# Sixteen experts as four rounds of four, in plain fp32 on 32-column tiles of the tensor engine

## The chip, the cores and the metric

The kernel runs on one core of a Trainium2 chip. A core has five engines that work side by side, each through its own instructions in the order in which the program gives them: TensorE (PE; its weight loads stand as PEld), VectorE (DVE), ScalarE (ACT), GpSimd (POOL) and SyncE (SP). Transfers between HBM and the on-chip memory are issued by SP, POOL and ACT and carried out by 16 DMA engines. The metric is the device time of one execution in microseconds (us).

## What is computed

One encoder layer on x of 512 tokens by 1024, all float32. First x grows by two mixers (attention and a bidirectional state space model, through w_in, w_attn_o, w_ssd_o and w_out); then by a mixture of 16 experts on the normed tokens h2:

```
h2 = rmsnorm(x, norm_ffn_w)
# a router takes one of 4 groups, and in it 2 of 4 experts, for each token
for e in range(16):
    y_e = (silu(t @ w1[e]) * (t @ w3[e])) @ w2[e]     # 1024 -> 512 -> 1024
    out = out + combine[:, e:e + 1] * y_e
```

Each token has two experts, so the 16 experts have 64 tokens each on average. The kernel gives every expert a list of CAP = 96 places; a general path behind the stage serves experts with more tokens, and it is skipped here. The experts' weights are 96 MB of float32: 192 pieces of 512 KB.

## The kernel before

**Order.** All work up to the end of the expert stage is written as jobs, `job(engine, us, emit, after, take, free, prio)`, of the class Plan (L122 to L210). Plan.run (L171) puts them in order on a model of the engines: each job has a time, a load has 1.0 us more (DLAT), two engines are 0.2 us apart (LAT), and rooms are counted ("e" for weights, "G" for gathered tokens, "whl" for split weights, "ys" for results). Of the jobs of an engine, the one that can start earliest goes next, and among equals the one of the lowest prio. The order that comes out is the program; on the chip each engine keeps it and waits at any instruction whose inputs are late, whatever stands behind it.

**Precision.** A float32 product is made of three passes in the faster type fp32r: a weight piece is split by ACT into a rounded high part (L1333) and by DVE into the rest (L1337), tokens likewise (L1628, L1632), and mm3 (L266) multiplies high by high, high by low, low by high (L267 to L269).

**The expert stage**, one expert after another. The stationary operand is the tokens' 128 x 96 block, the moving one a 128 x 512 block of weights. up_mm makes u = t @ w1 and v = t @ w3 (8 blocks of 128 rows each), g_silu and g_mul make the gated product, q_mmt transposes it, down_mm makes y (4 blocks, two halves of 512). An expert has 24 such products of three passes, 72 matmuls of 512 columns; the stage has 1152. Each expert's weights are 12 pieces, and the planner keeps the u and v of an expert ahead of the down product of the one before.

**Tokens.** h2 is stored to HBM (h2_d, L1406, four transfers of 512 KB by POOL). The first two experts' tokens come by a product with one-hot lists (pg_first, L1473); those of the other 14 by an indirect gather of 96 rows on POOL (L1620) into one of NG = 3 rooms, and eight transposes of a block on PE (L1625). Lists come from s_oh, s_mm, s_ix (L1601 to L1613). The results go out by an indirect scatter that adds to HBM (L1676, 16 of 96 rows), from a single room.

**Weights** are loaded by SP (eload, L1682) into 18 rooms of their own, 3 of an older pool and 12 in the places of tiles that are done with (`more`, L1704); a room is free when its piece has been split. w1 and w3 pieces have rows of 2 KB, w2 pieces of 4 KB.

Of the kernel before, what the change touches and what calls it, by code (L numbers as in the profile page):

```python
# [11 lines left out]
F32 = mybir.dt.float32  # L12
F32R = mybir.dt.float32r
BF16 = mybir.dt.bfloat16
I32 = mybir.dt.int32
# [22 lines left out]
# numbers of buffers  # L38
# [16 lines left out]
# model of the engines: delay between two, after a load; between dependent steps of one  # L55
# [8 lines left out]
ONEHOT = 2  # L64
TG = ((0, 2), (2, 3), (3, 4))
WARM = 36
# interval of the tensor engine's clock, load of an activation table
# [10 lines left out]
PGP = (320, 2015)  # L78
PGB = (('sc', 'sc'), ('tp', 'tp'))
# [30 lines left out]
class Late:  # L110
    """a tile that takes its buffer at its first use"""
# [10 lines left out]
class Plan:  # L122
    """jobs of one engine each, put in order on a model of the engines (time of a job, a delay between engines,
    buffers that jobs take and give back); of the jobs that can start, the one of the lowest prio goes first"""
# [36 lines left out]
    def clock(self, t, us, duty):  # L161
        """the end of a job of the tensor engine: at half its clock in an interval that follows an idle one"""
# [51 lines left out]
def tile_block(ctx: ExitStack, tc: tile.TileContext, x, norm_mix_w, w_in, b_gate, q_norm_w, k_norm_w,  # L214
# [18 lines left out]
    # ---------------------------------------------------------------- helpers  # L233
# [16 lines left out]
    def rsqrt(y, v, n, eps=EPS):  # L250
        """steps of a reciprocal square root"""
# [19 lines left out]
    # ---------------------------------------------------------------- x, constants  # L271
# [9 lines left out]
    def a2(nm, dt=F32, pat=None, **kw):  # L281
# [4 lines left out]
                 "a2": NA2 - 6, "eb": 3, "ab": 2, "a4": 2, "qa": 3, "cbm": 2, "gat": 0, "e": 0, "u": 2, "H": 2, "Q": 1, "G": NG, "ys": 1, "sl": 1})  # L286
# [18 lines left out]
    # ---- loads of the first part, in the order in which they are needed  # L305
# [27 lines left out]
    def warm(n):  # L333
        """keeps the clock of the tensor engine up"""
# [67 lines left out]
    # ---- first norm  # L402
# [54 lines left out]
    # ---- token-major projections: keys, values, step sizes; queries  # L457
# [75 lines left out]
    # ---- constants  # L533
# [4 lines left out]
    def rope_w():  # L538
        """steps of the factors of the rotation, with the weights of the norms and the scale of the scores in them"""
# [21 lines left out]
    rc = cp.tile([P, NT, NE, 5], BF16, name="rc")  # L561
# [3 lines left out]
    def router_c():  # L565
        V.tensor_copy(rc[:, :, :, 0:2],
                      cst[:, C_TC:C_TC + 8].rearrange("p (t j) -> p t j", j=2).unsqueeze(2).to_broadcast([P, NT, NE, 2]))
# [10 lines left out]
    # ---- norm and rotation of queries and keys  # L578
# [45 lines left out]
    # ---------------------------------------------------------------- from the other projections to the merge  # L624
# [11 lines left out]
    # ---- stream of weights: 128 output channels at a time  # L636
# [101 lines left out]
    # ---- step sizes, decays  # L738
# [79 lines left out]
    # ---- keys  # L818
# [36 lines left out]
    # ---- the projections themselves  # L855
# [25 lines left out]
    # ---- SSD states  # L881
# [43 lines left out]
    # ---- SSD outputs  # L925
# [37 lines left out]
    def ssd_dt(c, d):  # L963
        """x times its step size, per direction"""
# [132 lines left out]
    # ---- attention  # L1097
# [123 lines left out]
    # ---- gates, merge  # L1221
# [31 lines left out]
    # ---- buffers of the second half: a part takes the room of an earlier one when that is done  # L1253
# [7 lines left out]
    def room_q():  # L1261
# [4 lines left out]
        t_["s"] = ep.tile([P, DE], F32, tag="s", name="s_e")  # L1266
# [8 lines left out]
    # ---------------------------------------------------------------- second residual, norm, router  # L1275
# [9 lines left out]
    def room(i, *shapes):  # L1285
        """parts of a tile of the router's room"""
# [12 lines left out]
    sqj_, lgs, oh0a, oh0b, beat, pr, wn, lg, mx5, sm5, go, df, wsum, gv = room(  # L1299
        1, [256], [2 * P], [NT, CAP], [NT, CAP], [NT * 5, 4, 4], [NT * 5, 4], [NT * 5, 4], [NT, 20], [NT * 5], [NT * 5], [NT, 4],  # L1300
# [4 lines left out]

    def oh0(e):
        return (oh0a, oh0b)[e]()
# [20 lines left out]
    def piece(nm, prio, load, k, n, take, give, deps, sp):  # L1328
        """a piece of weights: its load and its two parts"""
# [47 lines left out]
    def logits(t, kb):  # L1377
        """channels in four column groups of the tensor engine, to be summed"""
# [36 lines left out]
    def topk(t0, t1):  # L1415
        """steps of the choice of a group and of two experts in it, for a range of tokens"""
# [33 lines left out]
    # position of every token in every expert's list: routed tokens upwards from 0, the others downwards from S - 1  # L1450
# [13 lines left out]
    # tokens of the first experts, by a matrix product with their one-hot slots  # L1464
    def oh_first(e, t):
        V.tensor_tensor(oh0(e)[:, t, :], iota[:, :CAP], slot[:, t, e:e + 1].to_broadcast([P, CAP]), op=ALU.is_equal)

    def pg_first(e, t, kb):
        if t == 0:
            t_["pg", e, kb] = bank(PGB[e][kb], "pg%d_%d" % (e, kb))  # L1470
            T.matmul(t_["pg", e, kb], lhsT=onb, rhs=zb[:, 0:1].to_broadcast([P, 512]), start=True, stop=False)
        for j in range(4):
            T.matmul(t_["pg", e, kb][:, j * P:j * P + CAP], lhsT=us(t)[:, (kb * 4 + j) * P:(kb * 4 + j + 1) * P],  # L1473
                     rhs=oh0(e)[:, t, :], start=False, stop=(t, j) == (NT - 1, 3))

    # weight of every token for every expert, in exact bf16 parts
    def weigh():
# [3 lines left out]
        def w3(a):  # L1481
            return a.unsqueeze(2).to_broadcast([P, NT, NE])
        return [(0.14, lambda: V.tensor_tensor(cw, prv()[:, :, 4:20], mk, op=ALU.mult)),
# [410 lines left out]
```

## Time and profile before

| | us |
|---|---|
| median of 3 runs (lowest, highest) | 691.66 (691.45, 691.82) |
| span of the profiled execution | 691.8 |
| expert stage, first to last matmul | 389.7 to 677.8 |
| PE busy in the stage | 287.7 |
| last matmul to the end | 14.0 |

No time of its own is given for the profiled execution beyond its span; the span agrees with the runs to 0.1 to 0.3 us. A page of the profile gives busy time by engine, then the span in 40 slices of 17.3 us; a slice's digit is the busy share in tenths. The clock row shows which share of full speed TensorE was granted, the DMA row the mean share of the 16 DMA engines. Timeline rows give start, duration, engine, line, operation and operands of each instruction, and in brackets the idle time before it with what ended it.

### The profile page before, as it was taken

How to read it: one execution, taken by the hardware profiler on the slowest of the kernel's cores; microseconds unless marked ns; L12 is line 12 of the kernel's file. 1: busy time of each engine (PE TensorE's matmuls, PEld its weight loads, DVE VectorE, ACT ScalarE, POOL GpSimd, SP SyncE). 2: the span in 40 equal slices, each digit the busy share in tenths (PEclk: the TensorE clock that was granted, in tenths of full speed). 3: DMA queues.
4: the chain of work that ended last, by engine and by line, in shares of the span. 5: the costliest groups of instructions: out<-in, count | busy, mean ns of one | idle time of the engine just before them, and what ended most of it. 6: DMA issues, size and time to landing. Idle time of an engine off the chain costs nothing. (4 is left out here: it accounts for less than half of the span.)

```text
span 691.8 us, 10208 instructions
## 1 busy us (share of the span) xinstructions
PE 669.1 (97%) x3609; PEld 517.9 (75%) x3611; DVE 553.7 (80%) x877; ACT 463.2 (67%) x689; POOL 96.5 (14%) x118
## 2 busy tenths in 40 slices
PE   7899999999999999999999999999999999999991
PEld 5788887777888888888777877777777777777761
DVE  4679968978699996566526899999999999999981
ACT  5445555777568779433435478888888888888870
POOL 4624100222000000000012102011111111100001
PEclk9999999999999999999999999999999999999996
DMA  8721732565221012897638999999999999999613
GB/s 278 195 65 38 178 90 66 151 182 124 61 62 40 24 51 67 278 340 259 252 118 278 366 357 338 367 375 365 363 363 361 362 361 359 362 377 376 244 23 48
DMA packets 96043, 155.04 MB, mean 224 GB/s; under 512 B 8680, under 2 KB 45044, under 8 KB 95988
## 3 DMA queue, kind: packets, MB, share of 16 engines
q1 hardware_dynamic: 87076, 131.79, 55.3%
q0 software_dynamic: 6848, 22.49, 12.8%
q8 instruction: 29, 0.48, 0.3%
q10 hardware_dynamic: 2064, 0.07, 0.2%
q14 instruction: 26, 0.21, 0.1%
HBM read 143.74 MB, written 10.58 MB: 223 GB/s over the span
## 5 line engine op out<-in xcount | busy, mean ns | idle before, releaser
L267 PE MATMUL b<-hTh,wc_hi 128*128 128x512 f32 x208 | 85.3, 410 | 0.0
L269 PE MATMUL b<-hTh,wc_lo 128*128 128x512 f32 x208 | 82.1, 395 | 0.0
L268 PE MATMUL b<-hTl,wc_hi 128*128 128x512 f32 x208 | 82.1, 395 | 0.0
L657 ACT ACTIVATE wc_hi<-wc_r 128x1024 fp32r<-128x1024 f32 x34 | 35.9, 1057 | 29.8 <-PE b L268 16.3
L661 DVE TENSOR_TENSOR wc_lo<-wc_r,wc_hi 128x1024 fp32r<-128x1024 f32 x34 | 41.5, 1223 | 8.8 <-ACT wc_hi L657 8.5
L1676 POOL DMA_INDIRECT out_dram<-GY,ixe x16 | 27.9, 1746 | 144.1 <-ACT GY L1673 138.4
L267 PEld LDWEIGHTS b<-hTh,wc_hi 128*128 128x128 f32 x208 | 39.0, 188 | 10.4 <-issue 1.5
L269 PEld LDWEIGHTS b<-hTh,wc_lo 128*128 128x128 f32 x208 | 39.0, 187 | 9.5
L268 PEld LDWEIGHTS b<-hTl,wc_hi 128*128 128x128 f32 x208 | 39.1, 188 | 7.7
L1337 DVE TENSOR_TENSOR whl<-ve_r,whl 128x1024 fp32r<-128x1024 f32 x25 | 30.6, 1223 | 3.9 <-ACT whl L1333 3.0
L1333 ACT ACTIVATE whl<-ve_r 128x1024 fp32r<-128x1024 f32 x25 | 26.5, 1058 | 8.5 <-PE pue L269 8.5
L1337 DVE TENSOR_TENSOR ue_lo<-ue_r,ue_hi 128x1024 fp32r<-128x1024 f32 x24 | 29.3, 1221 | 3.1 <-ACT ue_hi L1333 2.9
L1620 POOL DMA_INDIRECT GY<-h_d,ixe x14 | 14.4, 1026 | 117.5 <-PE pge L1625 99.1
L1333 ACT ACTIVATE ue_hi<-ue_r 128x1024 fp32r<-128x1024 f32 x24 | 25.3, 1055 | 3.5 <-PE y1e L269 2.6
L1337 DVE TENSOR_TENSOR whl<-ue_r,whl 128x1024 fp32r<-128x1024 f32 x21 | 25.6, 1221 | 1.0 <-ACT whl L1333 1.0
L1333 ACT ACTIVATE whl<-ue_r 128x1024 fp32r<-128x1024 f32 x21 | 22.3, 1061 | 6.1 <-PE y1e L269 4.1
L1337 DVE TENSOR_TENSOR we_lo<-we_r,we_hi 128x1024 fp32r<-128x1024 f32 x21 | 25.6, 1221 | 0.7
L267 PE MATMUL pve<-whl,H 128*96 128x512 f32 x64 | 26.1, 408 | 0.0
L1333 ACT ACTIVATE we_hi<-we_r 128x1024 fp32r<-128x1024 f32 x21 | 22.3, 1062 | 5.6 <-PE pve L269 4.5
L267 PE MATMUL pue<-whl,H 128*96 128x512 f32 x64 | 25.9, 404 | 0.0
L1157 DVE TENSOR_TENSOR PTl<-ppt,PTh 128x512 fp32r<-128x512 f32 x32 | 21.6, 687 | 4.8 <-ACT PTh L1152 4.5
L267 PE MATMUL pue<-ue_hi,H 128*96 128x512 f32 x64 | 25.3, 396 | 0.0
(400 smaller groups left out, 2069.9 us busy)
## 6 DMA issues: line engine op xcount, KB each, us to landing
ue_r<-in_w_dram SPq DMA_DIRECT2D x45, 512.0 KB, 12.2
ve_r<-in_w_dram SPq DMA_DIRECT2D x44, 512.0 KB, 9.8
we_r<-in_w_dram SPq DMA_DIRECT2D x39, 512.0 KB, 12.3
wc_r<-in_w_in_dram SPq DMA_DIRECT2D x26, 512.0 KB, 5.0
EXx<-in_w_dram SPq DMA_DIRECT2D x22, 512.0 KB, 12.2
EXm<-in_w_dram SPq DMA_DIRECT2D x22, 512.0 KB, 11.7
EXr<-in_w_dram SPq DMA_DIRECT2D x20, 512.0 KB, 12.7
x<-in_x_dram SPq DMA_DIRECT2D x8, 512.0 KB, 6.8
```

What stands on the lines that cost most here:

```text
L267: T.matmul(ps, lhsT=lh, rhs=rh, start=first, stop=False)
L268: T.matmul(ps, lhsT=lh, rhs=rl, start=False, stop=False)
L269: T.matmul(ps, lhsT=ll, rhs=rh, start=False, stop=last)
L657: A.activation(t_["w", i][0], t_["raw", i], AF.Copy)
L661: V.tensor_tensor(l_, t_.pop(("raw", i)), h_.bitcast(F32), op=ALU.subtract)
L1157: V.tensor_tensor(PTl[:, :, q2], t_.pop(("pt", u)).rearrange("p (k q) -> p k q", k=NT), PTh[:, :, q2].bitcast(F32), op=ALU.subtract)
L1333: A.activation(t_["w", nm][0], t_["raw", nm], AF.Copy)
L1337: V.tensor_tensor(l_, t_.pop(("raw", nm)), h_.bitcast(F32), op=ALU.subtract)
L1620: G.indirect_dma_start(g[:n], None, h2_d, bass.IndirectOffsetOnAxis(ap=t_["ix", nm][:n, 0:1], axis=0))
L1676: G.indirect_dma_start(out, bass.IndirectOffsetOnAxis(ap=t_["ix", nm][:n, 0:1], axis=0), y_buf()[:n], None, compute_op=ALU.add)
```

## The change

A round q (four of them) takes four experts at once, 4*j+q for j = 0 to 3, each in a 32-column tile j of the tensor engine: the stationary operand is 32 tokens of expert j (RN = 32), the moving operand a raw float32 block of its weights, and the output the partitions 32j to 32j+31 of one bank. Each list of 96 has NR = 3 parts r, so a block of weights of four experts is passed three times. A job of up_mm or down_mm is four such plain matmuls. Per round there are 24 jobs for u, 24 for v and 12 for each half of y: 288 in all. Nothing is split: L1333 and L1337 go from the stage, the tokens' splits too, and one copy (t_out, s_out) takes the place of each pair. A group of four weight rooms is freed by the last part's job (spent) instead of by a split. All pieces have rows of 2 KB; the w2 pieces are halves of the output's columns. Rooms are 35 (18, 3, two in EXm, four each in EXx, EXr and the new EXu).

The stage's order is a list of 16 phases, in which u of a round is put ahead of y of the round before. Only part (0, 0) comes by one-hot products; the other 11 parts come by gathers of 128 rows into NG = 2 rooms, taken in turn, and 12 scatters of 128 rows leave from three rooms. The transposes of round q have the prio just below v of round q-1.

```diff
 NE4 = 18
-NG = 3
...
+NG = 2
...
+RN = 32
+NR = CAP // RN
+NQ = 4
...
+    def oh_first(t):
+        V.tensor_tensor(oh0()[:, t, :].rearrange("p (j i) -> p j i", j=4), iota[:, 0:RN].unsqueeze(1).to_broadcast([P, 4, RN]),
+                        slot[:, t, :].rearrange("p (j q) -> p j q", q=NQ)[:, :, 0:1].to_broadcast([P, 4, RN]), op=ALU.is_equal)
+    def pg_first(t, kb):
         if t == 0:
...
+            t_["pg", kb] = bank("sc", "pg%d" % kb)
+            T.matmul(t_["pg", kb], lhsT=onb, rhs=zb[:, 0:1].to_broadcast([P, 512]), start=True, stop=False)
         for j in range(4):
...
+            T.matmul(t_["pg", kb][:, j * P:(j + 1) * P], lhsT=us(t)[:, (kb * 4 + j) * P:(kb * 4 + j + 1) * P],
+                     rhs=oh0()[:, t, :], start=False, stop=(t, j) == (NT - 1, 3))
...
+    pgj = {0: [], 1: []}
+    for t in range(NT):
+        j_ = job("dve", 0.17, lambda t=t: oh_first(t), [j_slot[t]], prio=PGP)
+        for kb in range(2):
+            pgj[kb] = [job("pe", 1.0 + 0.22 * (t == 0), lambda t=t, kb=kb: pg_first(t, kb), [j_, j_us[t]] + pgj[kb],
+                           ["sc"] if t == 0 else [], prio=PGP, duty=0.9)]
...
+    ohp = [cp.tile([P, NT, P], BF16, name="oh_%d" % i) for i in range(NR)]
+    TH = [Late(h8, "TH%d" % i, F32, "p (a k s) -> p a k s", a=2, k=KD) for i in range(NR)]
+    GS = [Late(a8, "GS%d" % i, F32, "p (a n) -> p a n", a=2) for i in range(2)]
+    YS = [Late(lambda nm, i=i: whl.tile([P, 1024], F32, tag=("hi", "lo")[i % 2], name=nm), "YS%d" % i) for i in range(4)]
+    def T_(q, r):
+        i = (q % 2) * NR + r
+        return TH[i // 2][:, i % 2]
+    def g_buf(R):
+        return GS[0][:, R % NG, :]
+    def y_buf(r):
+        return YS[r][:, :]
+    def s_buf(r):
+        return (YS[3][:, 0:512], YS[3][:, 512:1024], GS[1][:, 0, 0:512])[r]
+    def sT_(r):
+        return (GS[1][:, 0, 512:1024], GS[1][:, 1, 0:512], GS[1][:, 1, 512:1024])[r].rearrange(K4, k=4)
...
+    def gather(g, i):
+        G.indirect_dma_start(g, None, h2_d, bass.IndirectOffsetOnAxis(ap=i, axis=0))
...
+    def t_mm(q, r, kb):
+        g = g_buf(NR * q + r)
+        pt = t_["pg", q, r, kb] = bank("tp", "pg%d_%d_%d" % (q, r, kb))
         for j in range(4):
...
+            T.transpose(pt[:, j * P:(j + 1) * P], g[:, (kb * 4 + j) * P:(kb * 4 + j + 1) * P], ident)
+    def t_out(q, r, kb, src):
+        o, i = T_(q, r)[:, kb * 4:kb * 4 + 4, :], src.rearrange(K4, k=4)
+        if kb:
+            V.tensor_copy(o, i)
+        else:
+            A.activation(o, i, AF.Copy)
...
+    def up_mm(x_, q, r, k, tag):
+        if k == 0:
+            t_["p", x_, q, r] = bank(tag, "p%s%d_%d" % (x_, q, r))
         for j in range(4):
...
+            js = slice(j * RN, (j + 1) * RN)
+            T.matmul(t_["p", x_, q, r][js, :], lhsT=T_(q, r)[:, k, js], rhs=t_["raw", x_, q, k // 2, j][:, k % 2, :],
+                     start=k == 0, stop=k == KD - 1)
+    def down_mm(h, q, r, k, tag):
         if k == 0:
...
+            t_["p", h, q, r] = bank(tag, "py%s%d_%d" % (h, q, r))
+        for j in range(4):
+            js = slice(j * RN, (j + 1) * RN)
+            T.matmul(t_["p", h, q, r][js, :], lhsT=sT_(r)[:, k, js], rhs=t_["raw", h, q, k // 2, j][:, k % 2, :],
+                     start=k == 0, stop=k == 3)
+    def spent(x_, q, kk):
+        for j in range(4):
+            t_.pop(("raw", x_, q, kk, j))
+            ebufs.append(t_.pop(("buf", x_, q, kk, j), r4))
...
+    def scatter(q, r):
...
+        G.indirect_dma_start(out, bass.IndirectOffsetOnAxis(ap=sx[q][:, r:r + 1], axis=0), y_buf(r), None, compute_op=ALU.add)
...
+    def source(x_, e, kk):
+        if x_ in "uv":
+            return (w1v if x_ == "u" else w3v)[e][:, kk * 2:kk * 2 + 2, :]
+        return w2v[e][:, kk * 2:kk * 2 + 2, int(x_) * 512:(int(x_) + 1) * 512]
...
+    more(h8, "EXm", [j_rooms])
...
+        more(g8, "EXu%d" % i, j_h2[2 * i:2 * i + 2] + pgs)
...
+    phases = [("u", 0), ("v", 0), ("u", 1), ("0", 0), ("1", 0), ("v", 1), ("u", 2), ("0", 1), ("1", 1), ("v", 2), ("u", 3),
+              ("0", 2), ("1", 2), ("v", 3), ("0", 3), ("1", 3)]
+    at = {ph: 2000 + 100 * i for i, ph in enumerate(phases)}
+    jw, jT, jti, jsT, jy, jmul, jgx = {}, {}, {}, {}, {}, {}, {}
+    for x_, q in phases:
+        for kk in range(4 if x_ in "uv" else 2):
+            for j in range(4):
+                key = (x_, q, kk, j)
+                jw[key] = last["e"] = job(
+                    "dma", 1.46, lambda key=key: eload(key, source(key[0], 4 * key[3] + key[1], key[2])),
+                    [j_rq] + ([last["e"]] if "e" in last else []), ["e"], prio=1000 + len(jw), lat=DLAT)
...
+    def sl_jobs(q):
+        o = at["v", q - 1] - 130 if q else 700
+        rs = list(range(NR))
+        oh = [job("dve", 0.6, lambda r=r: s_oh(q, r), [j_slot[t] for t in range(NT)] + (jti.get(q - 1, [])[:1]),
+                  prio=o + (0 if r else 15) * (q == 0)) for r in rs]
...
+        jti[q] = [k_, j_]
+        for r in rs:
+            if (q, r) != (0, 0):
+                k_ = job("pool", 1.03, lambda r=r: gather(g_buf(NR * q + r), ix[q][:, r:r + 1]), [jx, j_rooms] + j_h2,
+                         ["G"], prio=o + r)
+                jgx[q, r] = job("dma", 1.3, lambda: None, [k_], prio=-500, lat=DLAT)
+    def t_jobs(q):
+        o = at["v", q - 1] - 20 if q else 1900
+        for r in range(NR):
+            jT[q, r] = []
+            for kb in range(2):
+                tk = ["T"] * (kb == 0)
+                if (q, r) == (0, 0):
+                    k_, free = pgj[kb], ["sc"]
+                else:
+                    k_ = [job("pe", 0.55, lambda r=r, kb=kb: t_mm(q, r, kb), [jgx[q, r]] + jT[q, r], ["tp"],
+                              ["G"] if kb else [], prio=o + r, duty=0.5)]
+                    free = ["tp"]
+                jT[q, r] = jT[q, r] + [job(
+                    "dve" if kb else "act", 0.6 if kb else 0.48,
+                    lambda r=r, kb=kb: t_out(q, r, kb, t_["pg", kb] if (q, r) == (0, 0) else t_["pg", q, r, kb]),
+                    k_ + [j_rooms], tk, free, prio=o - 1500)]
+    def up_jobs(x_, q, prev):
+        o, tags = at[x_, q], ("sc", "sc", "sc") if x_ == "v" else ("mm", "mm", "ac")
+        nk = KD
+        order_ = [(r, k) for k in range(nk) for r in range(NR)]
+        if (x_, q) == ("u", 0):
+            order_.sort(key=lambda o_: (o_[0] > 0, o_[1]))
+        if (x_, q) == ("v", NQ - 1):
+            order_.sort(key=lambda o_: o_ if o_[1] >= nk - 2 else (-1, o_[1]))
+        for n, (r, k) in enumerate(order_):
+            dep = [jw[x_, q, k // 2, j] for j in range(4)] + jT[q, r] + prev
+            end = (r, k % 2) == (NR - 1, 1)
+            def f(r=r, k=k, end=end):
+                up_mm(x_, q, r, k, tags[r])
+                if end:
+                    spent(x_, q, k // 2)
+            prev = [job("pe", 0.857, f, dep, [tags[r]] if k == 0 else [],
+                        (["e"] * 4 if end else []) + (["T"] if x_ == "v" and k == nk - 1 else []), prio=o + n)]
+            if k == nk - 1:
+                p_ = o - 1500
+                if x_ == "u":
+                    jmul[q, r] = job("act", 0.6, lambda r=r: g_silu(q, r), prev + [j_top[NT - 1]], ["s"], [tags[r]], prio=p_, tab="silu")
+                else:
+                    k_ = job("dve", 0.6, lambda r=r: g_mul(q, r), prev + [jmul[q, r]], [], [tags[r]], prio=p_)
+                    k_ = job("pe", 0.64, lambda r=r: s_t(q, r), [k_], ["tp"], ["s"], prio=o + 130 + r if q < NQ - 1 else o, duty=0.5)
+                    jsT[q, r] = job("act", 0.48, lambda r=r: s_out(q, r), [k_], ["sT"], ["tp"], prio=p_)
+        return prev
+    def y_jobs(q, r, h, ks, tag, o, prev):
+        end = ks[-1] == 3
+        for k in ks:
+            def f(k=k):
+                down_mm(h, q, r, k, tag)
+                if r == NR - 1 and k % 2:
+                    spent(h, q, k // 2)
+            prev = [job("pe", 0.857, f, [jw[h, q, k // 2, j] for j in range(4)] + [jsT[q, r]] + prev, [tag] if k == 0 else [],
+                        (["e"] * 4 if r == NR - 1 and k % 2 else []) + (["sT"] if h == "1" and k == 3 else []), prio=o)]
+        if end:
+            hi = int(h)
+            jy[q, r, hi] = job("dve" if hi else "act", 0.6, lambda: y_ev(h, q, r, hi), prev + [jti[q][1]],
+                               ["ys"] if hi == 0 else [], [tag], prio=o - 1500)
+            if hi:
+                k_ = job("pool", 1.03, lambda: scatter(q, r), [jy[q, r, 0], jy[q, r, 1]], prio=o)
+                job("dma", 1.3, lambda: None, [k_], free=["ys"], prio=-400, lat=DLAT)
+        return prev
...
+    for q in range(NQ):
+        sl_jobs(q)
+        t_jobs(q)
```

The jobs not shown here (the lists of a round, the evacuations y_ev, the silu and the products) are as before, on 128 partitions instead of 96; the scatters follow the evacuations of their part. The last loops add the phases in their order: in a y phase of rounds 0 to 2 the blocks k run outside and the parts r inside.

## Rows read from the trace of the kernel before

**Rows 1.** The page: busy time by engine; DMA share in 40 slices.

```profile
PE 669.1 (97%) x3609; PEld 517.9 (75%) x3611; DVE 553.7 (80%) x877; ACT 463.2 (67%) x689; POOL 96.5 (14%) x118
...
DMA  8721732565221012897638999999999999999613
```

**Rows 2.** Windows: engines' busy us (instructions), granted clock, DMA share, GB/s; the stage.

```profile
389.70:677.80 288.10, 287.72 (x1425) 205.39 (x1422) 265.44 (x299) 237.05 (x280) 40.30 (x29) 1.00 0.96 331
```

**Rows 3.** Timeline of PE near the stage's end: start, duration, instruction.

```profile
660.17 0.39 PE L268 MATMUL pve<-whl,H 128*96 128x512 f32 x1
...
661.79 0.39 PE L269 MATMUL pve<-ve_hi,H 128*96 128x512 f32 x1
```

**Rows 4.** Windows: the last loads, and the end after them.

```profile
600.00:651.00 51.00, 51.00 (x245) 36.44 (x244) 47.22 (x47) 44.24 (x53) 5.16 (x3) 1.00 1.03 371
651.00:692.00 41.00, 26.42 (x118) 17.88 (x116) 22.02 (x21) 19.76 (x24) 4.81 (x3) 0.86 0.21 35
```

**Rows 5.** Groups by line and form: the two splits of one weight piece.

```profile
L1337 DVE TENSOR_TENSOR ue_lo<-ue_r,ue_hi 128x1024 fp32r<-128x1024 f32 x24 | 29.3, 1221 | 3.1 <-ACT ue_hi L1333 2.9
...
L1333 ACT ACTIVATE ue_hi<-ue_r 128x1024 fp32r<-128x1024 f32 x24 | 25.3, 1055 | 3.5 <-PE y1e L269 2.6 <-PE pve L269 0.6 <-PE px L269 0.3
```

**Rows 6.** Timeline of the kernel's end.

```profile
679.83 0.68 ACT L1673 ACTIVATE GY<-y0e,tie 96x512 f32<-96x512 f32 x1 [4.98 <-DMA out_dram<-GY,ixe]
...
681.56 1.42 POOL L1676 DMA_INDIRECT out_dram<-GY,ixe  x1 [5.68 <-DVEq L1832]
```

**Rows 7.** Timeline of PE around a product on 32-column tiles.

```profile
342.06 0.40 PE L269 MATMUL px<-wt_hi,mTl 128*128 128x512 f32 x1
342.38 0.43 PE L1383 MATMUL plg<-lp,wr 128*32 128x128 f32 x8
342.74 0.66 PE L1368 MATMUL ph<-cst,x 128*128 128x128 f32 x4
343.15 0.48 PE L267 MATMUL px<-wt_hi,mTh 128*128 128x512 f32 x1
```

**Rows 8.** Timeline of PE around a product on two tiles at a time.

```profile
109.88 1.51 PE L892 MATMUL st<-xw,B_tok 128*64 128x256 f32 x12
111.32 0.50 PE L267 MATMUL b<-hTh,wc_hi 128*128 128x512 f32 x1
```

**Rows 9.** Timeline of all engines at the stage's start.

```profile
385.00 0.17 DVE L1462 TENSOR_TENSOR slot<-slot,plt 128x16 f32<-128x16 f32 x1 [0.57 <-PE plt L1497]
...
387.71 2.00 PE L1473 MATMUL pg<-lp,us 128*128 128x96 f32 x16
...
388.27 0.56 DVE L1632 TENSOR_TENSOR H<-pg,H 128x384 fp32r<-128x384 f32 x1
...
389.12 1.03 POOL L1620 DMA_INDIRECT GY<-h_d,ixe  x1 [10.10 <-DVE nxf L1813]
...
389.72 0.46 PE L267 MATMUL pue<-whl,H 128*96 128x512 f32 x1
```

**Rows 10.** DMA issues: engine, count, KB of each, median us to landing.

```profile
ue_r<-in_w_dram SPq DMA_DIRECT2D x45, 512.0 KB, 12.2
...
out_dram<-GY,ixe POOLq DMA_INDIRECT x16, 8.3
GY<-h_d,ixe POOLq DMA_INDIRECT x14, 7.5
```

**Rows 11.** DMA issues in 378 to 379 us: the last store of h2.

```profile
h_d<-us POOLq DMA_DIRECT2D x1, 512.0 KB, 8.4
```

**Rows 12.** Groups by line: the scatters on POOL.

```profile
L1676 POOL DMA_INDIRECT out_dram<-GY,ixe x16 | 27.9, 1746 | 144.1 <-ACT GY L1673 138.4 <-DVEq L1832 5.7
```

**Rows 13.** Windows around PE's idle stretches, early and before the stage.

```profile
23.00:25.12 2.12, 0.03 (x1) 0.00 (x0) 2.12 (x2) 1.54 (x2) 2.12 (x2) 1.00 0.18 65
...
25.38:28.79 3.41, 3.41 (x17) 3.41 (x17) 3.22 (x6) 3.12 (x4) 3.05 (x5) 0.51 0.57 113
...
372.00:377.00 5.00, 3.71 (x29) 3.10 (x34) 4.07 (x17) 3.63 (x8) 1.12 (x2) 1.00 1.07 332
```

More of the change, by code (lines that the diff above doesn't have):

```diff
@@ L77 @@
 PQW = 5882
-PGP = (320, 2015)
-PGB = (('sc', 'sc'), ('tp', 'tp'))
+PGP = 320
 PR = -1749
@@ L560, in rows_out @@
         V.tensor_copy(pc, t_["pst"][:, :R_N])
-    rc = cp.tile([P, NT, NE, 5], BF16, name="rc")
+    rc = cp.tile([P, NT, NQ, 18], BF16, name="rc")
+    msk = cp.tile([P, 4], F32, name="msk")
+    spare = cp.tile([P, 1], F32, name="spare")
     tkd = cp.tile([P, NT], F32, name="tkd")
@@ new lines, in T_, with rooms @@
+    def T_(q, r):
[9 more added lines that the diff above has]
+        return (GS[1][:, 0, 512:1024], GS[1][:, 1, 0:512], GS[1][:, 1, 512:1024])[r].rearrange(K4, k=4)
+    def rooms():
+        for t in TH + GS:
+            t[:, 0]
+        for t in YS:
+            t[:, 0:512]
@@ new lines, in s_oh, with s_mm @@
+    def s_oh(q, r):
+        V.tensor_tensor(ohp[r].rearrange("p t (j i) -> p t j i", j=4),
+                        iota[:, r * RN:(r + 1) * RN].unsqueeze(1).unsqueeze(1).to_broadcast([P, NT, 4, RN]),
+                        slot.rearrange("p t (j q) -> p t j q", q=NQ)[:, :, :, q:q + 1].to_broadcast([P, NT, 4, RN]),
+                        op=ALU.is_equal)
+    def s_mm(nm, q, rs, n):
+        t_["pi", nm] = bank("tp", "pi" + nm)
+        for r in rs:
+            for t in range(NT):
+                T.matmul(t_["pi", nm][:, r * 18:r * 18 + n], lhsT=ohp[r][:, t, :], rhs=rc[:, t, q, 0:n], start=(t == 0),
+                         stop=(t == NT - 1))
@@ L1804, in tile_block @@
-    d_jobs(NE - 1, q_jobs(NE - 1), weights_e(NE - 1, "w"))
+    wo_all = [j for t in range(NT) for j in j0[t]] + [j for kq in range(4) for j in w1_[kq]]
+    j_rooms = job("any", 0.0, rooms, wo_all, lat=0.0)
+    uts = [js[t][n][i] for t in range(NT) for n in range(2) for i in (2, 3)]
+    pgs = pgj[0] + pgj[1]
+    more(h8, "EXm", [j_rooms])
+    for i in range(2):
+        more(g8, "EXx%d" % i, [j for t in (2 * i, 2 * i + 1) for n in range(2) for j in js[t][n]] + j_us[2 * i:2 * i + 2]
+             + j_st[2 * i:2 * i + 2])
@@ new lines, in sl_jobs, with step @@
+    def sl_jobs(q):
[3 more added lines that the diff above has]
+                  prio=o + (0 if r else 15) * (q == 0)) for r in rs]
+        if q == 0:
+            k_ = job("pe", 0.4, lambda: s_mm("a", q, rs[1:], 2), oh[1:], ["tp"], prio=o, duty=0.1)
+            jx = job("dve", 0.2, lambda: s_ix("a", q, rs[1:]), [k_], free=["tp"], prio=o)
+        nm = "q%d" % q
+        k_ = job("pe", 0.5, lambda: s_mm(nm, q, rs, 18), oh + [j_w5] + ([jx] if q == 0 else []), ["tp"], prio=o + 5, duty=0.1)
+        j_ = k_
+        if q:
+            jx = j_ = job("dve", 0.2, lambda: s_ix(nm, q, rs), [k_], prio=o)
+        tis = []
+        def step(i):
+            if not tis:
+                tis.extend(s_ti(nm, q))
+            tis[i][1]()
+        for i in range(NR + 6):
+            j_ = job("dve", 0.09, lambda i=i: step(i), [j_], free=["tp"] if i == NR + 5 else [], prio=o + 6)
+        jti[q] = [k_, j_]
+        for r in rs:
+            if (q, r) != (0, 0):
+                k_ = job("pool", 1.03, lambda r=r: gather(g_buf(NR * q + r), ix[q][:, r:r + 1]), [jx, j_rooms] + j_h2,
+                         ["G"], prio=o + r)
+                jgx[q, r] = job("dma", 1.3, lambda: None, [k_], prio=-500, lat=DLAT)
```

371 lines of the change are left out of this document (126 added, 245 removed).

## The prediction

> **What bounds the kernel now.** I read the page's busy times and slices first: TensorE is busy for 669.1 of the span's 691.8 us, and the DMA digits are 9 from the 22nd slice to the 37th, so two resources look full in the last half [rows 1]. Windows over the expert stage separate them: from the first product at 389.7 to the last at 677.8 PE is busy 287.72 of 288.10 us at clock 1.00 [rows 2], and the timeline shows its matmuls back to back, seven steps of 512 columns from 660.17 to 661.79, 1.62 / 7 = 0.2315 us each [rows 3]. The weights flow at a DMA share of 1.03 until 651, and after that at 35 GB/s [rows 4]: PE needs 27 us more than the loads do, with no wait for them. The splits (1.055 us on ACT, 1.221 on DVE for one of 192 pieces [rows 5]: 203 and 234 us) fit beside 288 us of PE. So PE sets the stage; loads are the next bound, some 20 us behind. At the end ACT evacuates 2.0 us after PE's last matmul, having waited for the previous scatter to leave the single result room; the last scatter starts at 681.56 [rows 6], and 14.0 us pass from PE's last matmul to the span's end.
>
> **The products.** Before: 1152 matmuls x 0.2315 = 266.7 us; the rest of 288.1, 21.4 us, is transposes, lists and exits. After: 288 jobs of four tiles. Two places of the trace show plain fp32 on column tiles. Eight instructions of 128 columns on 32-column tiles (four tiles, two instructions to a matmul, so two steps if the four run together) take 342.38 to 342.74 = 0.36 us [rows 7]; twelve of 256 columns, two tiles at a time, six steps, take 109.88 to 111.32 = 1.44 us [rows 8]. With a cost a per column and b per exit, 256a + b = 0.36 and 1536a + b = 1.44: a = 0.844 ns, b = 0.144 us. A 512-column step is 0.432 us, a job 0.864, the stage's 288 jobs 248.8 us: -17.9. If the four tiles did not overlap, [rows 7] would need 8 x 128 x 0.844 = 864 ns and show 360.
>
> **Around the products.** Transposes are groups of four: 11 gathered parts x 2 and 4 x 3 products = 34 groups; the neighbouring group of four took 342.74 to 343.15 = 0.41 [rows 7], so 13.9 us. Each time PE leaves tile work and returns costs an entry of 0.32 - 0.23 = 0.09 [rows 7] and the exit b = 0.144, 0.23 us; some 30 returns are 6.9. The lists' 12 small groups of matmuls cost an estimated 2 us, under half of that 0.41 each. PE work: 248.8 + 13.9 + 6.9 + 2 = 271.6 against 288.1: -16.5. Bounds of the job: with no exit at all [rows 8] alone give 1.44 / 1536 = 0.94 ns and 0.96 us (276.5 in all, +28 on the sum); with an exit as long as a whole step of [rows 3], 0.23, they give 0.79 ns and 0.81 us (-16). [Rows 7] alone would give 1.41 ns, 1.44 us a job and +166; [rows 8], nearer in columns, exclude it. I take the solved value, the only one that fits both. Product transposes that head a phase and wait for their evacuations on DVE: +2 (0 to 5).
>
> The splits' 203 and 234 us leave ACT and DVE; nothing waited for them, so nothing is gained there, and 0.5 us copies replace them. Rooms come free by groups of four, after the third pass, instead of by a split; 35 instead of 33 make up for it, and loads had a margin of 27 us [rows 4], so nothing, or up to +5 where the first round fills them.
>
> **Start.** The 16 one-hot products of the second expert take 2.00 us from 387.71, and a split of 0.56 at 388.27 ends ahead of the first product at 389.72 [rows 9]. Both go: the first job about 387.2, -2.5 (-4 to 0). **End.** Three result rooms instead of one take away ACT's 2.0 us at the end [rows 6], but three scatters of the last round stand close together: -1.7 (-2 to +4).
>
> Without waits this is 691.8 - 16.5 - 2.5 - 1.7 + 2 = 673. The loads' own floor: last landing at 651 + some 4 us for rooms, six jobs behind the last group 5.2, 14 us of end: 674. They would meet.
>
> **The waits.** The planner expects a gathered part 1.03 + 1.3 + 1.0 + two times 0.2, that is 3.7 us after its issue, up to 1.46 more behind a load. On the chip a gather of 96 rows took 7.5 us to landing (median of 14), with the queues as full as they will be again [rows 10]. PE keeps its order, so a transpose that the plan put four jobs behind the issue holds all matmuls after it. Before, three rooms let gathers be issued an expert ahead. Now the third part of each round uses the room of the first (NG = 2), so its gather can be issued only when the first part's transposes are done, and those stand at the head of the very phase in which the third is wanted. Four places:
>
> - u of round 0, parts 1 and 2: the last store of h2 is issued at 378.46 and needs 8.4 [rows 11], landing 386.9; gather out at 387.4, landing 7.6 + 0.4 later for a third more rows, 395.4. PE begins at 387.2 and after four jobs and some lists is there at about 391.3: 4.0.
> - v of round 0, part 2 of round 1: 8.3 us from room to tokens, against two transposes and four or five jobs, 4.9: 3.5.
> - v of rounds 1 and 2, the third parts of rounds 2 and 3: as above, but three scatters have come to POOL's queue at the end of the phase before, each 1.75 us on POOL [rows 12] and 8.3 to landing [rows 10]. The plan counts 1.3 for each, so it puts eight or nine jobs (7.3 us) between; the gather lands some 13 us after: 5.5 each, 2 to 10.
>
> Sum 18.5 us (8 to 30). What hides a part of it: nothing on PE; a wait in front of PE only fills rooms.
>
> **The clock.** After PE was idle for 2.12 us its clock was granted at 0.51, the lower of its two levels, for the next 3.41 us [rows 13]: 1.7 us lost. After the 1.29 us of idle between 372 and 377 it stayed at 1.00 [rows 13]. Three to four waits over 2 us lose 5.2 to 6.8 us; I take 5.7.
>
> Forecast: 673 + 18.5 + 5.7 = 697 us. Its span and the median of the runs before differ by 0.1, which I neglect.
>
> **The rivals.**
> 1. *Waits mostly absent*, faster. The plan's own PE may stall for a group of four loads, and then transposes of a later round go ahead early, with their gathers; the order that comes out can't be read from the diff. For it: loads and PE nearly balance (674 to 673), so small gaps exist in the plan; in the trace of before no wait for a gather is seen [rows 2]. Against: rooms are full at the stage's start. One wait of 4 us and its clock left (1.7) gives 673 + 5.7 = 679; 673 to 683. It decides from the point where waits and clock together are under 691.8 - 673 = 19 us. A gather that lands in 4 us instead of 7.5 would end there too. DMA: Bandwidth & Descriptors in the Trainium skill (Anatomy of one DMA, SWDGE path) has 2.0 us and the bytes at 436 GB/s, an estimated 3.2 us for 128 rows of 4 KB, and 674 for the kernel; the 7.5 us of [rows 10], on queues filled by loads, disagrees.
> 2. *The four tiles share something at 512 columns*, slower. The price is in the job: from 0.864 + 18.7 / 288 = 0.93 us on, all that is saved without waits is gone; at the bound of 0.96 it is 697 + 28 = 725 with the waits and 701 without. For it: no row has four tiles at 512 columns. Against: one line through [rows 7, 8] with whole overlap. TensorE: Matmul & The Clock Gate in the Trainium skill (Part 3, packing) speaks against the change: three column tiles at 512 columns ran 2.38 times as fast as one after another, 0.79 of the full three. By it a job would be an estimated 0.864 / 0.79 = 1.09 us and the kernel some 66 us later than by the rows; the 0.36 us of [rows 7] disagrees, at 128 columns.
> 3. *Scatters hold the gathers longer*: 10 us at each of two places instead of 5.5, and one more of the kind: 706 to 715.
> 4. *Loads decide*: rooms given back by fours and held longer make PE wait for weights all along, which takes up the gather waits: 674 + 4 to 16 = 678 to 690. For it: share 1.03 for 250 us [rows 4].
>
> **How the numbers follow.** Chances: the forecast (686 to 706) 0.42, rival 1 0.31, rival 2 0.08, rival 3 0.11, rival 4 0.08. About 0.2% (1.4 us) is what a measurement can tell from no change. Of the forecast's case 0.05 lie under 690.4 and 0.08 within 1.4 of the time before. Faster by more: rivals 1 and 4 and that 0.05, 0.44. Within: 0.08. Slower: the forecast's other 0.29 and rivals 2 and 3, 0.48. The range of 8 in 10 reaches from inside rival 1 to the middle of rival 3, 674 to 711; the forecast's own is 686 to 706.
>
> **What would show it.** Jobs: eight tile matmuls each 0.86 us, with PE's sum some 16 us less than [rows 2]; a job over 0.93 would refute the first term. Waits: in PE's list of what it waits for, four groups of 2 us and more that end with a gather's landing (through the transposes), each followed by a stretch at clock 0.5. If PE's idle time in the stage is under 5 us, or its idle time ends with weight loads instead, the forecast is wrong and rival 1 or 4 holds. ACT and DVE should fall to under a quarter of their 237 and 265 us in the stage [rows 2], with nothing gained by it.

## The result: 729.4 us, slower by 5.4%, and the profile after

The changed kernel's median is 729.44 us (726.77 to 731.37, four runs) beside 691.74 for the kernel before on the same chip: a ratio of 1.0541, 95% interval 1.0516 to 1.0566. The forecast was 697 us, range 674 to 711: the direction was right, the size by far not. The profiled execution took 731.37 us, the longest of the four, with a span of 729.6; the sums below are made in spans, against 691.8.

The page of the changed kernel, for [rows 1]: busy times, and PE's busy share in 40 slices of 18.2 us.

```profile
PE 655.1 (90%) x4635; PEld 400.1 (55%) x4637; DVE 319.6 (44%) x663; ACT 248.4 (34%) x450; POOL 85.5 (12%) x111
...
PE   6999999999999999999997989992799919999970
```

PE is busy for 90% of the span instead of 97%; slices 28 and 33 have holes (2 and 1 tenths). Windows over the stage (382.75 to 707.7, for [rows 2]) and over four stretches, each right behind a wait of PE; the columns are those of [rows 2].

```profile
382.75:707.70 324.95, 280.04 (x2491) 90.49 (x2488) 37.72 (x102) 27.21 (x47) 27.24 (x21) 0.92 0.86 296
393.38:397.63 4.25, 4.25 (x20) 1.28 (x20) 0.00 (x0) 0.60 (x1) 0.00 (x0) 0.55 0.38 70
424.56:428.00 3.44, 3.44 (x16) 1.28 (x20) 0.00 (x0) 0.60 (x1) 0.00 (x0) 0.51 1.05 388
514.83:520.40 5.57, 5.57 (x28) 2.07 (x32) 0.00 (x0) 0.60 (x1) 0.00 (x0) 0.53 0.01 3
603.18:608.90 5.72, 5.71 (x28) 2.09 (x32) 0.00 (x0) 0.60 (x1) 0.00 (x0) 0.50 0.00 0
```

The stage lasts 324.95 us instead of 288.10, with PE busy for 280.04. What PE waited for (us in all, times, longest):

```profile
PE pg L1662 <- DMA GS<-h_d,ix: 43.3, 4, 17.9
```

So 43.3 of the 44.9 idle us are four waits for gathered tokens. The rows with which the other three end, then PE around the first (timeline, for [rows 3] and [rows 7]):

```profile
424.56 0.66 PE L1662 MATMUL pg<-cst,GS 128*128 128x128 f32 x2 [2.61 <-DMA GS<-h_d,ix]
...
514.83 1.09 PE L1662 MATMUL pg<-cst,GS 128*128 128x128 f32 x4 [17.87 <-DMA GS<-h_d,ix]
...
603.18 1.09 PE L1662 MATMUL pg<-cst,GS 128*128 128x128 f32 x4 [17.59 <-DMA GS<-h_d,ix]
```

```profile
393.38 1.09 PE L1662 MATMUL pg<-cst,GS 128*128 128x128 f32 x4 [5.22 <-DMA GS<-h_d,ix]
...
400.54 13.94 PE L1677 MATMUL pu<-u,TH 128*32 128x512 f32 x128
414.41 1.09 PE L1662 MATMUL pg<-cst,GS 128*128 128x128 f32 x8
```

128 instructions, 16 jobs, start at 400.54 and are followed at 414.41: 13.87 / 16 = 0.867 us a job. Now POOL around the first long wait: the second and third gather of round 2 (L1656) and, between them, the scatters of round 0 (L1709); then the last three scatters. The brackets say what ended POOL's idle time.

```profile
479.27 0.94 POOL L1656 DMA_INDIRECT GS<-h_d,ix  x1 [0.30 <-issue]
486.86 1.64 POOL L1709 DMA_INDIRECT out_dram<-YS,sx  x1 [6.65 <-DVE YS L1846]
497.40 1.55 POOL L1709 DMA_INDIRECT out_dram<-YS,sx  x1 [8.90 <-DMA out_dram<-YS,sx]
506.99 1.55 POOL L1709 DMA_INDIRECT out_dram<-YS,sx  x1 [8.04 <-DMA out_dram<-YS,sx]
508.84 1.02 POOL L1656 DMA_INDIRECT GS<-h_d,ix  x1 [0.30 <-issue]
...
705.85 1.55 POOL L1709 DMA_INDIRECT out_dram<-YS,sx  x1 [23.74 <-DVE YS L1846]
712.81 1.55 POOL L1709 DMA_INDIRECT out_dram<-YS,sx  x1 [5.41 <-DMA out_dram<-YS,sx]
719.61 1.55 POOL L1709 DMA_INDIRECT out_dram<-YS,sx  x1 [5.24 <-DMA out_dram<-YS,sx]
```

This is what I had not seen. Scatters of one round are ready together, and each starts only when the one before has landed (497.40 and 506.99 after idle times of 8.90 and 8.04 that a scatter's landing ended). They stand 10.5 and 9.6 us apart, and the gather of the third part is the next instruction on POOL: it leaves at 508.84, 29.6 us behind its neighbour of 479.27. The waiting is in the program: in front of each scatter POOL has a semaphore instruction of line L1709. At the end the same chain stands bare: 705.85, 712.81, 719.61. Landings (us from issue) of the first two of these scatters and of the gather behind them:

```profile
out_dram<-YS,sx POOLq DMA_INDIRECT x2, 9.3
```

```profile
GS<-h_d,ix POOLq DMA_INDIRECT x1, 5.8
```

The sum of the differences in span: the first product is 6.97 us earlier (382.75), the stage 36.85 longer, the end behind the last matmul 21.9 instead of 14.0, +7.9: 37.8, which is 729.6 - 691.8.

### The profile page after: what moved, and what is told of

The parts are those of the page before. It is cut to its first block, busy times and chain, and to the rows that moved or that the text cites. A ratio compares the mean times of both kernels' runs of the same rounds, so it can differ in the third digit from the quotient of the medians.

```text
span 729.6 us, 11444 instructions
## 1 busy us (share of the span) xinstructions
PE 655.1 (90%) x4635; PEld 400.1 (55%) x4637; DVE 319.6 (44%) x663; ACT 248.4 (34%) x450; POOL 85.5 (12%) x111
## 3 DMA queue, kind: packets, MB, share of 16 engines
q0 software_dynamic: 6800, 22.76, 12.3%
## 5 line engine op out<-in xcount | busy, mean ns | idle before, releaser
L1677 PE MATMUL pu<-u,TH 128*32 128x512 f32 x528 | 65.1, 607 | 0.0
L1677 PE MATMUL pv<-v,TH 128*32 128x512 f32 x372 | 64.1, 628 | 0.0
L1662 PE MATMUL pg<-cst,GS 128*128 128x128 f32 x88 | 15.4, 319 | 43.3 <-DMA GS<-h_d,ix 43.3
L1662 PEld LDWEIGHTS pg<-cst,GS 128*128 128x128 f32 x88 | 11.1, 162 | 57.6 <-issue 52.6
L1846 DVE TENSOR_SCALAR YS<-py,ti 128x512 f32<-128x512 f32 x12 | 9.0, 751 | 74.0 <-PE py L1685 73.7
L1677 PEld LDWEIGHTS pu<-u,TH 128*32 128x32 f32 x528 | 18.0, 112 | 38.3 <-issue 38.0
L1677 PE MATMUL pv<-EXx,TH 128*32 128x512 f32 x120 | 37.9, 614 | 0.0
L1709 POOL DMA_INDIRECT out_dram<-YS,sx x12 | 18.8, 1567 | 160.9 <-DVE YS L1846 95.6
L1677 PEld LDWEIGHTS pv<-v,TH 128*32 128x32 f32 x372 | 15.5, 113 | 30.8 <-issue 30.8
L1656 POOL DMA_INDIRECT GS<-h_d,ix x11 | 11.5, 1049 | 155.5 <-issue 117.6
```

Of the source, the lines that this page charges most:

```text
L1656: G.indirect_dma_start(g, None, h2_d, bass.IndirectOffsetOnAxis(ap=i, axis=0))
L1662: T.transpose(pt[:, j * P:(j + 1) * P], g[:, (kb * 4 + j) * P:(kb * 4 + j + 1) * P], ident)
L1677: T.matmul(t_["p", x_, q, r][js, :], lhsT=T_(q, r)[:, k, js], rhs=t_["raw", x_, q, k // 2, j][:, k % 2, :], start=k == 0, stop=k == KD - 1)
L1709: G.indirect_dma_start(out, bass.IndirectOffsetOnAxis(ap=sx[q][:, r:r + 1], axis=0), y_buf(r), None, compute_op=ALU.add)
L1846: V.tensor_scalar(o, i, w_, None, op0=ALU.mult)
```

## Experiments

Theory A: a scatter waits on POOL for the landing of the one before, because both add into one tensor; the third gather of a round stands behind three of them in POOL's order, and PE behind the gather. Theory B: indirect writes go one at a time whatever they write, or a gather lands late because loads fill the queues. Theory C, the prediction's: the room alone (NG = 2). Lines left out of an edit are marked with three dots. All times are medians of four runs (ten for e6, eight for e7); ratios stand against the kernel before.

**e1, three tensors.**

```diff
+    sc_1 = tc.dram_tile([S + P, D], F32, name="sc_1")
+    sc_2 = tc.dram_tile([S + P, D], F32, name="sc_2")
+    out_ = out
...
     def scatter(q, r):
+        out = (out_, sc_1, sc_2)[r]
```

> The three scatters of a round go to three tensors, parts 1 and 2 to scratch (so two thirds of the expert results are left out of the output); order, sizes and rooms stay. Theory A (a scatter waits on POOL until the one before it has landed, since both add into one tensor, and the third gather of a round stands behind three of them in POOL's order): spacing of scatters falls from 9.6 to 10.5 us to about 1.9, the two long waits of PE from 17.9 to under 4 each, the end after the last matmul from 22 to about 13; 689 us (684 to 697). Theory B (indirect writes go one at a time whatever they write, or land late because loads fill the queues): spacing and waits stay, 727 to 731. Theory C (the room alone, as forecast): waits are as long as before the edit, 727 to 731, only the end shrinks.

Measured: 701.44 us, ratio 1.0131 (1.0114 to 1.0148), over the range of 684 to 697. POOL, PE's waits and the third gather's landing:

```profile
485.10 1.64 POOL L1713 DMA_INDIRECT out_dram<-YS,sx  x1 [6.65 <-DVE YS L1850]
487.04 1.55 POOL L1713 DMA_INDIRECT sc<-YS,sx  x1 [0.30 <-ACT TH L1672]
488.90 1.55 POOL L1713 DMA_INDIRECT sc<-YS,sx  x1 [0.30 <-issue]
490.75 1.02 POOL L1659 DMA_INDIRECT GS<-h_d,ix  x1 [0.30 <-issue]
```

```profile
PE pg L1665 <- DMA GS<-h_d,ix: 22.0, 4, 8.0
```

```profile
GS<-h_d,ix POOLq DMA_INDIRECT x1, 12.3
```

With nothing else changed the scatters stand 1.9 us apart, and 28 us are gone. That rules out theory B's first half: the queue takes three scatters at once when they write to different tensors. PE's last matmul to the end takes 13.6 us instead of 21.9. But the longest wait is 8.0, not under 4: the gather, 18 us earlier on POOL, now has three scatters and the loads in flight beside it and takes 12.3 us, where it took 5.8 with the loads almost stopped. So the 689 missed by the term that theory B's second half names. What is left, 22.0 us of waits, is near the 18.5 of the forecast, and 701 near its 697.

**e2, only the place on PE.**

```diff
-                              ["G"] if kb else [], prio=o + r, duty=0.5)]
+                              ["G"] if kb else [], prio=o + r + 100 * (q > 0 and r == 2), duty=0.5)]
```

> Only the place of the third part's transposes in PE's order moves, one phase later (from behind 9 jobs of v to behind v). POOL's order and the scatters stay. Theory A: the gather still lands at about 515, PE arrives there after 24 jobs instead of 9, so 13 us of each long wait are covered by work, the short one of 2.6 goes: 729.4 - 26 - 2.6 - 1.7 = 699 (695 to 703), with two waits of 4 to 6 us left. Theory B: the same or less, up to 10 us more. If the waits were not what costs the time (clock or loads): 725 to 731.

Measured: 704.56 us, ratio 1.0173 (1.0154 to 1.0192), 1.6 over the range of 695 to 703. PE's waits, and the third scatter and the gather behind it:

```profile
PE pg L1662 <- DMA GS<-h_d,ix: 20.7, 3, 8.7
```

```profile
501.56 1.55 POOL L1709 DMA_INDIRECT out_dram<-YS,sx  x1 [8.59 <-DMA out_dram<-YS,sx]
503.41 1.02 POOL L1656 DMA_INDIRECT GS<-h_d,ix  x1 [0.30 <-PE pv L1677]
```

The gather is as late as before, behind the same scatters, and PE, with 15 more jobs ahead of it, waits 8.7 at most instead of 17.9. Work covered the wait, POOL did not change. The two long waits that are left are 8.4 and 8.7 us, where 4 to 6 were expected.

**e3, four rooms.**

```diff
-NG = 2
+NG = 4
...
+    GX = Late(h8, "GX", F32, "p (a n) -> p a n", a=2)
...
     def g_buf(R):
-        return GS[0][:, R % NG, :]
+        return (GS[0] if R % 4 < 2 else GX)[:, R % 2, :]
...
-    more(h8, "EXm", [j_rooms])
```

> Four rooms for gathered tokens instead of two, in the place of two rooms for weights (33 instead of 35); the planner then issues all gathers of a round ahead of the scatters. Theories A and C: PE's three later waits go (2.6 + 17.9 + 17.6) and some 2 us of low clock at each: 685 us (681 to 690), the end after the last matmul still 22. Theory B (late because queues are full): each gather still lands 8 to 10 us after its issue, PE waits 3 to 6 at each of three places, 695 to 702. If two rooms less starve PE of weights: waits for loads appear and it stays over 695.

Measured: 684.56 us, ratio 0.9887 (0.9871 to 0.9904). POOL, and all that PE still waited for tokens:

```profile
472.18 1.36 POOL L1658 DMA_INDIRECT GX<-h_d,ix  x1 [68.89 <-issue]
473.85 0.94 POOL L1658 DMA_INDIRECT GX<-h_d,ix  x1 [0.30 <-issue]
475.11 0.95 POOL L1658 DMA_INDIRECT GS<-h_d,ix  x1 [0.32 <-issue]
481.44 1.64 POOL L1711 DMA_INDIRECT out_dram<-YS,sx  x1 [5.38 <-DVE YS L1847]
491.78 1.55 POOL L1711 DMA_INDIRECT out_dram<-YS,sx  x1 [8.71 <-DMA out_dram<-YS,sx]
```

```profile
PE pg L1664 <- DMA GS<-h_d,ix: 3.7, 1, 3.7
```

Three gathers leave ahead of the first scatter, and of four waits the first, 3.7, is left. The scatters still stand 10.3 us apart, and nobody waits behind them until the end. Two rooms of weights less cost nothing that shows.

**e5, two rooms, earlier.** Lists, gathers and transposes of rounds 2 and 3 stand two phases earlier (with e2's edit):

```diff
-        o = at["v", q - 1] - 20 if q else 1900
+        o = at["v", q - 1] - (220 if q > 1 else 20) if q else 1900
...
-        o = at["v", q - 1] - 130 if q else 700
+        o = at["v", q - 1] - (330 if q > 1 else 130) if q else 700
```

> Two rooms as in the changed kernel, but lists, gathers and transposes of rounds 2 and 3 are placed two phases earlier, so that the third gather of a round leaves ahead of the scatters; third transposes one phase behind the first. Theory A (the gather's place behind the scatters): the three later waits go as with four rooms, 685 us (681 to 690), the first wait of 4 to 5 us and an end of 21 to 22 stay. Theory C (two rooms as such are too few): waits of 3 us and more stay at rounds 2 and 3, 693 to 700.

Measured: 683.83 us, ratio 0.9882 (0.9864 to 0.9899), the same as e3. PE's waits for tokens, and on POOL the third gather of round 2 with the row that follows it:

```profile
PE pg L1662 <- DMA GS<-h_d,ix: 5.1, 1, 5.1
```

```profile
464.98 0.95 POOL L1656 DMA_INDIRECT GS<-h_d,ix  x1 [23.60 <-PE pg L1662]
485.56 1.64 POOL L1709 DMA_INDIRECT out_dram<-YS,sx  x1 [19.64 <-DVE YS L1846]
```

The gather now leaves 20.6 us ahead of the first scatter. Two rooms are enough if the gathers leave ahead of the scatters. This ends theory C: e3's rooms helped by the order on POOL that they allowed.

**e4, the end.** The last round's y part after part, eight jobs each:

```diff
             ks = [(r, k) for k in range(4) for r in range(NR)]
             if x_ == "1":
...
+                continue
+            ks = [(r, h, k) for r in range(NR) for h in "01" for k in range(4)]
...
```

> The last round's y is made part after part (8 jobs each) instead of interleaved, so its three scatters can start 6.9 us apart. Theory A (they wait for one another): the end after PE's last matmul shrinks from 22 to 13 to 15 us: 721.5 us (719 to 724). If a scatter's landing alone sets the end: no change, 728 to 731. If the last weights come too late for this order: PE waits for loads at the end, 725 and more.

Measured: 716.95 us, ratio 1.0355 (1.0338 to 1.0373), below the range of 719 to 724. The last scatters:

```profile
691.89 1.55 POOL L1709 DMA_INDIRECT out_dram<-YS,sx  x1 [12.75 <-DVE YS L1846]
698.75 1.55 POOL L1709 DMA_INDIRECT out_dram<-YS,sx  x1 [5.31 <-DVE YS L1846]
705.62 1.55 POOL L1709 DMA_INDIRECT out_dram<-YS,sx  x1 [5.31 <-DVEq L1942]
```

They stand 6.9 us apart as before, now because eight jobs of PE lie between two of them, and the first two are under PE's work: last matmul to end 11.4 us instead of 21.9, in the spans, where 13 to 15 were expected. The gain of 12.5 us is more than forecast; 2 us of it lie ahead of the end, and I have no cause for them beyond the 726.8 to 731.4 over which the changed kernel's own runs spread.

**e6, the first wait.** Four rooms, and in round 0 part 0 goes through u and v (16 jobs) before the parts 1 and 2 go through either.

```diff
-                              ["G"] if kb else [], prio=o + r, duty=0.5)]
+                              ["G"] if kb else [], prio=o + r + 250 * (q == 0), duty=0.5)]
...
+        if q == 0 and x_ in "uv":
+            if x_ == "u":
+                for rs in ([0], [1, 2]):
+                    for w_ in "uv":
+                        prev = up_jobs(w_, 0, prev, rs)
...
```

> Four rooms, and the first part of round 0 runs through u and v (16 jobs) before the second and third parts are wanted. Wait of 3.7 us and some 2 us of low clock go if the first wait is what it looks like: 684.6 - 5.5 = 679 (676 to 682). If loads bound the kernel by now (share 1.05 from 400 to 650), the same time comes back as waits for weights: 683 to 686.

Measured: 691.03 us, ratio 0.9979 (0.9965 to 0.9993): 6.5 us slower than e3, over its range of 676 to 682 and over the 683 to 686 that it gave for binding loads. This order also loses tokens:

```profile
390.12 1.06 POOL L1658 DMA_INDIRECT GS<-h_d,ix  x1 [0.30 <-issue]
391.49 0.94 POOL L1658 DMA_INDIRECT GS<-h_d,ix  x1 [0.31 <-issue]
```

```profile
398.36 1.12 PE L1664 MATMUL pg<-cst,GS 128*128 128x128 f32 x4
```

GS has two rooms. Its first gather left at 383.05 (round 0, part 1); these two are of round 1, parts 1 and 2, and PE reads GS for the first time at 398.36. The plan counts free rooms without naming them, and round 1's transposes now go ahead of round 0's, so the last of the three gathers writes into the room of the first: round 0's part 1 is left out, and another part's tokens stand in its place, in e6, e7 and e8. Jobs and bytes are the same, but a kernel that kept the room would send that gather later, so the three times show what the order does to the loads and not what a complete kernel would take. Windows of this kernel and of e5 (as above, PE's busy us first), then its waits:

```profile
400.00:450.00 50.00, 49.40 (x446) 16.55 (x448) 5.42 (x8) 3.58 (x7) 0.00 (x0) 0.99 0.77 284
...
600.00:650.00 50.00, 46.20 (x369) 12.95 (x365) 4.32 (x6) 3.86 (x6) 4.66 (x3) 1.00 1.05 363
```

```profile
400.00:450.00 50.00, 50.00 (x468) 16.36 (x471) 10.60 (x33) 2.77 (x5) 5.60 (x5) 1.00 0.98 359
...
600.00:650.00 50.00, 49.25 (x456) 15.24 (x452) 4.32 (x6) 3.85 (x6) 4.66 (x3) 1.00 1.04 359
```

```profile
PE pv L1679 <- DMA v<-in_w_dram: 2.5, 5, 1.1
PE pg L1664 <- DMA GX<-h_d,ix: 2.4, 1, 2.4
```

The one wait left for tokens is 2.4, and it is for round 1's first gather. But a group of weights is given back only after its third pass, and now u and v of round 0 are both held. The loads stand still for want of rooms (the next one is sent at 411.4, in e5 at 403.6; share 0.77 from 400 to 450, e5 has 0.98), and near the end PE runs into them: 369 instructions in the 50 us from 600 on, 456 in e5. The last matmul ends at 668.2 instead of 661.7 in e3. The loads, which were done 27 us ahead of PE before, have become the bound.

**e7 and e8** carry e6's order with two forms of the end, so their loads bind as well.

> As e6, and the second half of y of the last round part after part (4 jobs each): the three last scatters can start 3.5 us apart instead of 1.7. Theory A: the end shrinks by 3.4 us, PE waits 1 to 2 for the last weights: e6 minus 2, 677 (674 to 680).

> As e6, with the whole y of the last round part after part, as in e4 (8 jobs each). If loads come in time the end shrinks by 8 to 12: 671. But the first part then wants all weights 14 us ahead of PE's last job, and they land about 6 us too late for that: 675 to 680 with PE waiting for loads near the end.

Measured: 690.34 us (0.9972, 0.9961 to 0.9983) and 688.61 (0.9949, 0.9931 to 0.9968): both missed with e6 (674 to 680 and 675 to 680 were expected). The end behind the last matmul is 18.2 and 11.5 us instead of 21.7, but the last matmul comes at 670.5 and 675.6 instead of 668.2, since the last weights are wanted earlier: what the end gives back is mostly lost again.

**e9 to e11, e5 with three orders of the end.**

> e5 and e4 together: rounds 2 and 3 gathered early, the last round's y part after part (8 jobs each). The last weights land at 651, and part 0 wants them at 647.4: PE waits 4 us, ends at 666 instead of 662, and the end behind it is 11.5 us instead of 21.5: 677.5 (675 to 681). If the three scatters did not wait for one another, only the 4 us would show: 688.

> As e9, but the first two blocks of the first half are made for all parts first (6 jobs), then 6 jobs a part. Last weights are wanted at 650.9, so PE hardly waits; scatters 5.2 us apart wait for one another for about 1.7 us each: end 15 us: 677.5 (675 to 681).

> As e9, but only the second half of y part after part (4 jobs each): scatters 3.5 us apart, two times 3.4 us of waiting left: 680 (678 to 682.5). The three orders then stand 677.5, 677.5, 680 and e5 at 683.8, if the price of the end is that a scatter waits for the landing of the one before.

Measured: 682.51 us (0.9857, 0.9832 to 0.9882), 681.94 (0.9846, 0.9823 to 0.9868) and 681.54 (0.9845, 0.9829 to 0.9862). The ends are as forecast, 11.4, 15.3 and 18.2 us behind the last matmul, but PE's last matmul comes at 669.2, 665.1 and 660.9 (662.0 in e5): 7 us later where each part is finished by itself. So e9 and e10 lie 1.5 and 0.9 us over their range of 675 to 681, and e11 lies in its own. The wait in e9 that e5 has not:

```profile
PE py L1685 <- DMA 13_0_2_5569<-in_w_dram: 2.7, 1, 2.7
```

The last weights are wanted earlier than they land, and the clock is granted at 0.85 and 0.81 in the 5 us around the wait and the 5 us after it. The three can't be told apart; e11 beats the kernel before by 10.6 us and the changed one by 48.

## Why the prediction was wrong

- **The products were right.** 0.867 us a job against 0.864. The Trainium skill's packing figure (TensorE: Matmul & The Clock Gate, Part 3), by which a job would be an estimated 1.09 us, does not hold for four column tiles of plain fp32 here: a step of all four took 0.433 us for 512 columns, and by the column that is no more than the two tiles at a time of [rows 8] (1.44 / 6 = 0.24 us for 256).
- **PE's work** was right, the clock a little short: stage less token waits 281.6 us, against 271.6 + 2 + 5.7 = 279.3. Behind the four waits PE ran at 0.50 to 0.55 for 4.3, 3.4, 5.6 and 5.7 us; by the granted clock some 9 us are lost there against the 5.7, which leaves 272.5 for the work against 273.6.
- **The start** was right for what it priced, and left something out: -7.0 against -2.5. Before, the last transposes for the router (ph) and the stage's first product stood at 375.27 and 389.72 ([rows 9] has the second); the rows of ph before and after:

```profile
375.27 0.63 PE L1368 MATMUL ph<-cst,x 128*128 128x128 f32 x4 [1.24 <-DVE lp L1437]
```

```profile
370.92 0.60 PE L1370 MATMUL ph<-cst,x 128*128 128x128 f32 x4
```

The two stand at 370.92 and 382.75 now, 11.83 us apart instead of 14.45. These 2.6 us are the forecast's, in part by luck: 64 one-hot products fewer are 6.1 us less of PE (9.6 against 15.7 in all), but PE now waits 1.7 us there for the router's last steps, and the last products ran at clock 0.53. The other 4.4 us are won ahead of that, in the mixers, where no job is edited. They had no term, and no run here shows their cause.

- **The waits were the step that failed**, and in it "three scatters have come to POOL's queue at the end of the phase before, each 1.75 us on POOL ... 5.5 each". The places were right, all four; the measured waits are 5.2, 2.6, 17.9 and 17.6 against 4.0, 3.5, 5.5 and 5.5: 43.3 instead of 18.5. A scatter does not hold POOL for 1.75 us if another follows: the second waits for the first one's landing (9.3 us, the median of two), and everything behind it waits too. Rival 3 had the direction but 10 us for it. The trace of before held the hint in [rows 6]: ACT's evacuation waited 4.98 us for a scatter's landing. I read it as the single result room, which three rooms would cure, and did not ask whether the next scatter would have waited as well. There scatters came one per expert, 288.1 / 16 = 18 us apart, so such a wait could not show. A count of what writes to one tensor within one landing time would have shown it.
- **The end** failed by the same step: 21.9 us against 12.3. Three rooms let the evacuations go on, the scatters not.
- The four differences, -4.5, +2.3, +24.8 and +9.6, are the 32 us between 697 and 729. The loads never bound the changed kernel: in its long waits it was the loads that stopped, for want of rooms (DMA share 0.01 and 0.00 right behind them).
- The rule of DMA: Bandwidth & Descriptors (Anatomy of one DMA, SWDGE path) in the Trainium skill, an estimated 3.2 us for such a gather, is not borne out either: the changed kernel's gathers took 4.3 us at the least, 5.8 where the loads had almost stopped, and e1's 12.3 behind three scatters.

Not tried: scatters into one tensor without their order. A token's two experts lie in one group and a round takes one expert of each group, so the scatters of one round add to different tokens' rows: by the lists the order inside a round protects nothing that the output needs. That is argued, not run. Open: why the changed kernel's runs spread over 4.6 us where those of the kernel before spread over 0.6 to 1.9; the longest of the four has the lowest granted clock (0.945) and the shortest the highest (0.956).

## What to carry to other kernels

Where the program orders transfers that add into one tensor, as here, they are a chain of landings, not of issues: price n of them that come together at n landings, and look at what stands behind them on their queue. The saving on the bounding engine (some 16 us here: 281.6 less 9 of clock, against 288.1) was only had once the transfers that feed it left ahead of that chain, which took three changed priorities. And a block of weights that is passed three times holds its room until the third pass: an order that puts off the wait for tokens (e6) turned into a wait for weights here. A plan that counts rooms without naming them is safe only in the order for which it was made: e6 lost a part's tokens that way.

## What the runs showed of the hardware

Four 32-column tiles of plain fp32 at 512 columns took 0.433 us a step (0.867 for eight instructions), by the column no more than two tiles at a time. A gather of 128 rows took 4.3 us at the least, 5.8 where the loads had almost stopped, and 12.3 behind three scatters with loads beside it. After idle times of 2.6 to 17.9 us PE ran at the lower clock level (0.50 to 0.55 over 3.4 to 5.7 us), in [rows 13] for 3.41 us after 2.12.
